# Output projections of a hybrid streaming layer: later weight pieces, and the first quarter block by block

## The chip, the cores and the metric

The kernel runs on one core of one Trainium2 chip. The metric is the device time of one execution in microseconds (us); lower is better. Instruction times below come from one profiled execution of the kernel before the change.

## What is computed

The reference is one trunk layer over 2048 prompt tokens and 32 sample tokens of another stream, with 1024 features:

```python
h = rms_norm(x, g_norm1) * (1 + scale1) + shift1
q, k, v, z, xbc_raw, dt_raw = split(h @ w_in)
attn = rms_norm(stick_breaking(norm(q), norm(k), v), g_attn_out)   # 8 heads of 64
ssm  = ssd_mixer(z, xbc_raw, dt_raw, ...)                           # 8 heads of 64, with its own rms_norm
x = x + gate1 * (concat([attn, ssm]) @ w_out)                       # the output projection
h2 = rms_norm(x, g_norm2) * (1 + scale2) + shift2
x = x + gate2 * ((silu(h2 @ w_gate) * (h2 @ w_up)) @ w_down)        # the feed-forward part, 2816 wide
```

The change concerns the line with `w_out` and its place among the work around it.

## The kernel before, in words

Every product is made of three matmuls on a high and a low part of each operand (`mm3`, lines 127 to 132). So each weight piece of 1 MB is first loaded raw into a buffer of the tag `wr` (two of them), and then split: ScalarE writes the high part `wh` and GpSimd (for `w_out` VectorE) the low part `wl`. There are three `wh`/`wl` pairs (`wtiles`, lines 72 to 78), and all the weights of the kernel take turns in them. A pair is free again when the last matmul that reads it is over.

The prompt is cut into four quarters of 512 tokens. After the input projection and the scan mixer, the stages are:

1. Attention of quarter 0, with the SSM half of quarter 0's output projection beside it (line 1605).
2. The rest of quarter 0's output projection, `run_all(w0.run())` (line 1614). It has to end before the feed-forward part can start, because that reads the normalised result `h2D` back from memory.
3. Two streams merged: `streamA` (attention of quarters 1 to 3 in `attn_w`, then `far_keys`, which adds the distant keys for those rows that need them, then the output projections of quarters 1, 2, the sample tokens and 3) and `streamF` (the feed-forward part of quarters 0 to 3).

**The order of the merged work** is set by `merge` (lines 1700 to 1726) and by a scheduler behind it. Each stream is a generator that yields a cost in nanoseconds after each piece of work it has written down. `merge` keeps a ledger: what streamA yields, times `ratio`, is owed to streamF; streamA is asked for its next piece when nothing is owed, streamF otherwise. After quarter 1's projection `ratio` is set to 4.0. The scheduler then places the instructions on the engines in about this order, each when its operands and buffers are there by its own estimate.

**The feed-forward part** (`ffn`, lines 885 to 993) goes through 11 groups per quarter. A group gets a piece of `w_gate`, of `w_up` and of `w_down`, computes two halves of 128 features (for each the products `pg` and `pu`, 24 matmuls each, yielding 5120), and then eight products `py` (6 matmuls each, yielding 1296). Pieces come from a queue (`Pieces`, lines 87 to 101) whose `get` hands out the oldest piece and at once calls for the next one. A group's `up` and `down` are thus called for when the group starts, and the next group's `gate` when its `py` start.

**One output projection** is an object `Wout` (lines 717 to 860). `pre` loads the mixed SSM rows (`mH`, `mL`), queues four pieces of `w_out` (two halves of the output columns for the SSM rows, two for the attention rows) and calls for the first (`self.pf.fill(1)`, line 735), and loads the gate rows `gr` and the residual rows `x1`. The tiles `gr` and `x1` lie in a pool on the memory that `streamA`'s attention tiles have just left. `ssm` makes the SSM products: for each half `hf`, for each of four token blocks `b`, 12 matmuls into a PSUM tile (`z`, or `d` in quarter 0), a VectorE instruction that scales it into `tm` (line 761), and a GpSimd addition into `x1` (line 763). `run` reads the attention rows, computes their norm, makes the same products for the attention half with a ScalarE sum of squares after each (line 852), and calls `norm2` for a block one block after its second half: it normalises the rows (lines 813 to 818), transposes them (line 825), writes `hx` with four ScalarE instructions for each half (line 831), splits it into `hl` and stores it to `h2D` (line 835). `hx` and `tm` share a tag of two buffers, and the two halves of `hl` have two buffers each.

`project` (lines 995 to 1000) runs `pre`, yields 3000, and then runs `ssm` and `run` for quarters 1 to 3 and for the sample tokens; quarter 0 is called from the top.

Of the kernel before, what the change touches and what calls it, by code (L numbers as in the profile page):

```python
# [35 lines left out]
def body(tc, nc, I, O):  # L36
    V, A, G, PE = nc.vector, nc.scalar, nc.gpsimd, nc.tensor
    ctx = ExitStack()
    with ctx:
# [12 lines left out]
        def load(dst, src):  # L52
            nc.sync.dma_start(dst, src)
# [73 lines left out]
        def mm3(out, pairs):  # L127
            n = len(pairs)
            for i, (sh, sl, mh, ml) in enumerate(pairs):
                PE.matmul(out, lhsT=sh, rhs=mh, start=(i == 0), stop=False)  # L130
                PE.matmul(out, lhsT=sh, rhs=ml, start=False, stop=False)  # L131
                PE.matmul(out, lhsT=sl, rhs=mh, start=False, stop=(i == n - 1))  # L132

        def mm2(out, pairs):

            n = len(pairs)
            for i, (s, mh, ml) in enumerate(pairs):
                PE.matmul(out, lhsT=s, rhs=mh, start=(i == 0), stop=False)
                PE.matmul(out, lhsT=s, rhs=ml, start=False, stop=(i == n - 1))

        def fold(dst, ps, n):
            A.activation(dst[:DEC, :n], ps[DEC:2 * DEC, :n], AF.Copy)
            V.tensor_tensor(dst[:DEC, :n], ps[:DEC, :n], dst[:DEC, :n], op=ALU.add)
# [573 lines left out]
        class Wout:  # L717
# [10 lines left out]
            def pre(self):  # L728

                s, t0 = self.s, self.t0  # L730
                mH, mL = mHL
                for i, t in enumerate((mH, mL if s == 0 else mH[:, :, DEC:])):
                    load(t[:, :, :self.n].bitcast(F32), mixT[i, :, :, t0:t0 + self.n].rearrange("k p t -> p k t"))
                self.pf = Pieces([lambda k=k, hf=hf, g=g: opiece(k, hf, g) for k, g in ((4, gsc), (0, gac)) for hf in range(2)])
                self.pf.fill(1)
                xsrc = I["x_prompt"][0, t0:t0 + self.n] if s == 0 else I["x_sample"][0]
                self.gr, self.x1 = [], {}
                for hf in range(2):
                    t = self.tile("gr", "gr")
                    load(t.rearrange("p (m c) -> p m c", m=4), modD[16 + hf * 4:20 + hf * 4, s].unsqueeze(0).to_broadcast([P, 4, P]))  # L740
                    self.gr.append(t)
                for b, c, m in self.tb:
                    x1 = self.tile("x1", "x1", nb=len(self.tb), w=D)
                    load(x1[:m], xsrc[c:c + m])
                    for hf in range(2):
                        self.x1[hf, b] = x1[:, hf * 512:(hf + 1) * 512]

            def product(self, hf, r):

                mH, mL = mHL  # L750
                wh, wl = self.pf.get()
                for b, c, m in self.tb:
                    ps = self.psum()
                    tm = self.tile("tm", "tm")
                    if self.s == 0:
                        mm3(ps[:m], [(mH[:, k, c:c + m], mL[:, k, c:c + m], wh[:, k, :], wl[:, k, :]) for k in range(4)])
                    else:
                        mm2(ps[:2 * DEC], [(mH[:, k, :2 * DEC], wh[:, k, :], wl[:, k, :]) for k in range(4)])
                        fold(tm, ps, 512)
                        ps = tm  # L760
                    V.scalar_tensor_tensor(tm[:m], ps[:m], r[:m, b:b + 1], self.gr[hf][:m], op0=ALU.mult, op1=ALU.mult)
                    x1 = self.x1[hf, b]
                    G.tensor_tensor(x1[:m], x1[:m], tm[:m], op=ALU.add)
                    yield b, tm
                    yield 12 * 216
# [72 lines left out]
            def run(self):  # L838
                yield from self.rows()
                nb, m0 = len(self.tb), self.tb[0][2]  # L840
                ra = sm.tile([P, 4], F32, tag="ra", name="ra", bufs=2)
                V.tensor_reduce(ra[:m0, :nb], stat[:m0, :, :nb].rearrange("p h b -> p b h"), axis=AX.X, op=ALU.add)
                rstd(ra[:m0, :nb], ra[:m0, :nb], 1.0 / 512, EPS)
                self.ss = {b: sm.tile([P, 2], F32, tag="s2", name="s2", bufs=8) for b, _, _ in self.tb}
                yield 1500
                lag = []
                for hf in range(2):
                    for x in self.product(hf, ra):
                        if isinstance(x, tuple):
                            b, tm = x  # L850
                            m = self.tb[b][2]
                            A.activation(tm[:m], self.x1[hf, b][:m], AF.Square, accum_out=self.ss[b][:m, hf:hf + 1])
                            continue
                        yield x
                        if hf == 1:
                            lag.append(self.tb[b])
                            if len(lag) > 1:
                                yield from self.norm2(*lag.pop(0))
                while lag:
                    yield from self.norm2(*lag.pop(0))  # L860
# [134 lines left out]
        def project(g, pool):  # L995
            w = Wout(g, pool, zps)
            w.pre()
            yield 3000
            yield from w.ssm()
            yield from w.run()  # L1000

# [597 lines left out]
        with ExitStack() as pb_:  # L1599
            mp = pb_.enter_context(tc.tile_pool(name="mp", bufs=1))  # L1600
            mHL, stat = mixed(mp)
            pw0 = ExitStack()
            w0 = Wout(0, pw0.enter_context(tc.tile_pool(name="wo0", bufs=1)), dense_ps)
            w0.pre()
            merge2(a0, w0.ssm(), R1)
            pa0.close()
            fc = px_.enter_context(tc.tile_pool(name="fc", bufs=1, side="right"))
            far_consts(fc)
            L = fc.tile([P, NH, 12], F32, name="L")
            px1 = ExitStack()  # L1610
            at1 = px1.enter_context(tc.tile_pool(name="at1", bufs=1, side="right"))
            wt = window_tiles(at1)
            a1 = chain(*(attn_w(g, at1, L, wt) for g in range(1, NQ)))
            run_all(w0.run())
            pw0.close()
            fp = pb_.enter_context(tc.tile_pool(name="fp", bufs=1))
            late = {}

            def streamA():
                yield from a1  # L1620
                yield from far_keys(at1, wt[0], L)
                px1.close()
                for g in range(1, NQ):
                    if g == 3:
                        yield from part_s()
                    with tc.tile_pool(name=f"wo{g}", bufs=1, side="right") as wo:
                        yield from project(g, wo)
                    if g < 3:
                        yield ("done", g)
                    if g == 1:  # L1630
                        yield ("ratio", 4.0)
                px_.close()
                late["ex"] = pb_.enter_context(tc.tile_pool(name="ex", bufs=1, side="right"))
                dpool[0] = pb_.enter_context(tc.tile_pool(name="pdF", bufs=5, space=PSUM))
                yield ("done", 3)

            def streamF():
                hT = load_h(0, fp, None)
                for g in range(NQ):
                    hT = yield from ffn(g, fp, late, hT)  # L1640

            merge(streamA(), streamF(), 1.55)


        fx = ctx.enter_context(tc.tile_pool(name="fx", bufs=1))
# [54 lines left out]
def merge(a, f, ratio):  # L1700
    done, debt = set(), 0.0
    a_live, f_live, need = True, True, None
    while a_live or f_live:
        blocked = a_live and need is not None and need not in done
        if not blocked:
            need = None
        if a_live and (blocked or not f_live or debt <= 0):
            try:
                c = next(a)
                if isinstance(c, tuple) and c[0] == "ratio":  # L1710
                    ratio = c[1]
                elif isinstance(c, tuple):
                    done.add(c[1])
                elif not blocked:
                    debt += c * ratio
            except StopIteration:
                a_live = False
        else:
            try:
                c = next(f)  # L1720
                if isinstance(c, tuple):
                    need = c[1]
                else:
                    debt -= c
            except StopIteration:
                f_live = False
# [29 lines left out]
```

## Time and profile before

| | us |
|---|---|
| median of three runs | 2942.09 |
| lowest, highest of the three | 2938.08, 2947.04 |
| the profiled execution | 2940.34 |
| its span, first to last instruction | 2938.4 |
| TensorE busy, of the span | 2729.8 (93%) |
| VectorE, ScalarE, GpSimd busy | 1563.9, 1186.0, 1532.6 |
| mean granted TensorE clock | 0.963 |

TensorE is busy for 93% of the span, so idle time of TensorE is what can be won, and it lies in a few places. Below, a row of the windows view gives for a stretch of time the busy microseconds of each engine with its number of instructions, then the granted TensorE clock, the busy share of the DMA engines and what they moved. A row of the timeline gives the start, the busy time (of several merged instructions where it ends in a number over x1), engine, line, operation, output and inputs, and in brackets how long the engine had been idle and what released it. `SPq` is the queue on which all these DMAs are issued.

### The profile page before, as it was taken

The page shows a single profiled execution, that of the slowest core. Times are in us where ns is not written, and L with a number is a line of the kernel's source. Part 1 is how long each engine was busy: PE and PEld are TensorE (multiplying, and loading weights), DVE is VectorE, ACT ScalarE, POOL GpSimd, SP SyncE. Part 2 cuts the span into 40 slices and gives each one's busy share as a digit, 9 for nine tenths or more (in the row PEclk, how much of TensorE's full clock was granted, in tenths as well). Part 3 has the DMA queues.
Part 4 walks back from the last instruction along what each step waited for, and adds up shares of the span by engine and source line. Part 5 has one row for each costly group of instructions (what it writes and reads, how often), then busy time and mean ns, then how long its engine had stood idle before and what let it go on. Part 6 is the DMA issues. An engine that isn't in the chain of part 4 may idle for free.

```text
span 2938.4 us, 41844 instructions
## 1 busy us (share of the span) xinstructions
PE 2729.8 (93%) x15467; PEld 2334.2 (79%) x15467; DVE 1563.9 (53%) x2575; ACT 1186.0 (40%) x2533; POOL 1532.6 (52%) x1318
## 2 busy tenths in 40 slices
PE   6998998998978689998879999999999999999998
PEld 5988997896977578876667887777787788899997
DVE  6577586766568567874344534434434422333336
ACT  6466365555535455522224334333243422322221
POOL 4767566564654635743136655544564445544445
PEclk8999998999988789999989999999999999999999
DMA  8755653463467787837745744534733722422221
GB/s 266 219 171 153 202 177 114 119 182 106 131 175 237 193 225 196 208 116 213 199 165 180 258 135 137 152 122 155 236 127 106 230 88 92 154 87 87 86 87 66
DMA packets 415619, 466.54 MB, mean 159 GB/s; under 512 B 34191, under 2 KB 330991, under 8 KB 415406
## 3 DMA queue, kind: packets, MB, share of 16 engines
q1 hardware_dynamic: 414478, 463.61, 52.7%
q8 instruction: 124, 2.03, 0.3%
q14 instruction: 89, 0.73, 0.1%
q10 hardware_dynamic: 896, 0.14, 0.0%
q0 software_dynamic: 32, 0.03, 0.0%
HBM read 372.66 MB, written 91.04 MB: 158 GB/s over the span
## 4 chain that ended last, share of the span: by engine, by line
PE 57%; DVE 6%; DMA 5%; issue 3%; POOL 2%; ACT 2%; SPq 1%; DVEq 0%; ACTq 0%; POOLq 0%
PE pg L130 5%; PE pg L131 5%; PE pg L132 5%; PE pu L130 5%; PE pu L131 5%; PE pu L132 5%; PE py L130 5%; PE py L131 4%; PE py L132 4%; PE z L130 2%; PE z L131 2%; PE z L132 1%; PE d L131 1%; PE d L130 1%; PE d L132 1%
## 5 line engine op out<-in xcount | busy, mean ns | idle before, releaser
L60 POOL TENSOR_TENSOR wl<-wr,wh 128x512 fp32r<-128x512 f32 x752 | 1010.3, 1375 | 861.7 <-ACT wh L59 778.5
L59 ACT ACTIVATE wh<-wr 128x512 fp32r<-128x512 f32 x816 | 450.3, 620 | 512.3 <-PE py L132 128.4
L130 PE MATMUL d<-wh,hH 128*128 128x256 f32 (+2 forms) x1088 | 316.0, 291 | 18.8 <-ACT hH L59 10.9
L132 PE MATMUL d<-wh,hL 128*128 128x256 f32 (+2 forms) x1088 | 311.8, 287 | 6.7 <-POOL hL L60 6.7
L130 PE MATMUL pg<-h,wh 128*128 128x512 f32 (+1 forms) x880 | 311.3, 354 | 3.7 <-POOL aT L378 2.5
L130 PE MATMUL pu<-h,wh 128*128 128x512 f32 (+1 forms) x880 | 310.5, 353 | 1.2 <-DVE sg L952 1.2
L131 PE MATMUL d<-wl,hH 128*128 128x256 f32 (+2 forms) x1088 | 311.4, 286 | 0.0
L132 PE MATMUL pg<-h,wl 128*128 128x512 f32 (+1 forms) x880 | 310.7, 353 | 0.6 <-POOL wl L60 0.6
L131 PE MATMUL pg<-h,wh 128*128 128x512 f32 (+1 forms) x880 | 310.7, 353 | 0.0
L132 PE MATMUL pu<-h,wl 128*128 128x512 f32 (+1 forms) x880 | 310.5, 353 | 0.0
L131 PE MATMUL pu<-h,wh 128*128 128x512 f32 (+1 forms) x880 | 309.9, 352 | 0.0
L130 PE MATMUL py<-wh,aH 128*128 128x512 f32 x704 | 282.5, 401 | 7.0 <-DVE ya L983 5.0
L131 PE MATMUL py<-wl,aH 128*128 128x512 f32 x704 | 277.0, 394 | 0.0
L983 DVE TENSOR_TENSOR ya<-py,ya 128x512 f32<-128x512 f32 x288 | 190.4, 684 | 148.4 <-PE py L132 146.8
L132 PE MATMUL py<-wh,aL 128*128 128x512 f32 x704 | 265.8, 394 | 2.8 <-DVE aL L60 2.8
L952 DVE TENSOR_TENSOR sg<-pg,sg 128x512 f32<-128x512 f32 (+1 forms) x110 | 64.8, 589 | 336.8 <-ACT sg L951 336.8
L130 PEld LDWEIGHTS d<-wh,hH 128*128 128x128 f32 (+1 forms) x1088 | 207.7, 191 | 23.2 <-ACT hH L59 12.5
L132 PEld LDWEIGHTS d<-wh,hL 128*128 128x128 f32 (+1 forms) x1088 | 206.9, 190 | 8.0 <-POOL hL L60 7.2
L131 PEld LDWEIGHTS d<-wl,hH 128*128 128x128 f32 (+1 forms) x1088 | 207.3, 191 | 0.7
L130 PEld LDWEIGHTS pg<-h,wh 128*128 128x128 f32 x880 | 165.6, 188 | 28.5 <-POOL aT L378 2.7
L130 PEld LDWEIGHTS pu<-h,wh 128*128 128x128 f32 x880 | 165.5, 188 | 24.2 <-DVE sg L952 1.4
L132 PEld LDWEIGHTS pg<-h,wl 128*128 128x128 f32 x880 | 165.4, 188 | 24.1 <-POOL wl L60 1.1
(434 smaller groups left out, 5686.7 us busy)
## 6 DMA issues: line engine op xcount, KB each, us to landing
wr<-in_w_in SPq DMA_DIRECT2D x48, 1024.0 KB
wr<-in_w_gate SPq DMA_DIRECT2D x44, 1024.0 KB
wr<-in_w_up SPq DMA_DIRECT2D x44, 1024.0 KB
wr<-in_w_down SPq DMA_DIRECT2D x44, 1024.0 KB
wr<-in_w_ada SPq DMA_DIRECT2D x24, 1024.0 KB
wr<-in_w_out SPq DMA_DIRECT2D x20, 1024.0 KB
h2D<-hl SPq DMA_DIRECT2D x64, 256.0 KB
Kw<-KT SPq DMA_DIRECT2D x48, 320.0 KB
```

What stands on the lines that cost most here:

```text
L59: A.activation(h, src, AF.Copy)
L60: (eng or V).tensor_tensor(l, src, h.bitcast(F32), op=ALU.subtract)
L130: PE.matmul(out, lhsT=sh, rhs=mh, start=(i == 0), stop=False)
L131: PE.matmul(out, lhsT=sh, rhs=ml, start=False, stop=False)
L132: PE.matmul(out, lhsT=sl, rhs=mh, start=False, stop=(i == n - 1))
L952: V.tensor_tensor(sg[:, :n], pg[:, :n], sg[:, :n], op=ALU.mult)
L983: V.tensor_tensor(dst, ps[:r], dst, op=ALU.add)
```

## The change

It does four things:

- `pre` calls for the first `w_out` piece only in quarter 0. In `project`, that is for quarters 1 to 3 and the sample tokens, the first piece is called for after a yield of 3500, and a second yield of 4500 follows before the SSM products, where there was one yield of 3000.
- In quarter 0, `run` takes both attention pieces of `w_out` from the queue at once and makes the products block by block: both halves of block 0, then of block 1, and so on. Before, all blocks of the first half came ahead of those of the second.
- `product` accepts a piece and a list of blocks for that.
- The ratio with which `merge` starts is 1.45 where it was 1.55.

```diff
@@ pre
                 self.pf = Pieces([lambda k=k, hf=hf, g=g: opiece(k, hf, g) for k, g in ((4, gsc), (0, gac)) for hf in range(2)])
-                self.pf.fill(1)
+                if self.g == 0:
+                    self.pf.fill(1)
@@ product
-            def product(self, hf, r):
+            def product(self, hf, r, w=None, tb=None):
 
                 mH, mL = mHL
-                wh, wl = self.pf.get()
-                for b, c, m in self.tb:
+                wh, wl = w or self.pf.get()
+                for b, c, m in tb or self.tb:
@@ run
                 lag = []
-                for hf in range(2):
-                    for x in self.product(hf, ra):
+                if self.g == 0:
+                    work = [self.pf.get() for _ in range(2)]
+                    work = [(hf, self.product(hf, ra, work[hf], [tb])) for tb in self.tb for hf in range(2)]
+                else:
+                    work = [(hf, self.product(hf, ra)) for hf in range(2)]
+                for hf, p in work:
+                    for x in p:
@@ project
             w.pre()
-            yield 3000
+            yield 3500
+            w.pf.fill(1)
+            yield 4500
             yield from w.ssm()
             yield from w.run()
@@ body
-            merge(streamA(), streamF(), 1.55)
+            merge(streamA(), streamF(), 1.45)
```

## The prediction

> **What bounds the kernel now.** First the page, for the share of each engine, then the windows view for where TensorE is not busy.
>
> ```profile
> span 2938.4 us, 41844 instructions
> ...
> PE 2729.8 (93%) x15467; PEld 2334.2 (79%) x15467; DVE 1563.9 (53%) x2575; ACT 1186.0 (40%) x2533; POOL 1532.6 (52%) x1318
> ```
>
> ```profile
> 1009.00:1048.00 39.00, 15.61 (x74) 12.68 (x72) 20.45 (x35) 25.89 (x60) 13.62 (x16) 0.60 0.89 266
> ...
> 1315.00:1402.00 87.00, 78.32 (x367) 62.27 (x366) 32.55 (x54) 21.33 (x44) 32.04 (x24) 1.00 0.74 198
> ...
> 1402.00:1460.00 58.00, 52.01 (x230) 41.11 (x228) 22.58 (x42) 12.91 (x26) 5.22 (x4) 0.94 0.81 230
> ...
> 1460.00:1496.00 36.00, 17.08 (x41) 10.22 (x40) 16.36 (x30) 0.26 (x1) 0.00 (x0) 0.65 0.54 182
> ...
> 1517.00:2925.00 1408.00, 1393.26 (x7065) 1165.89 (x7064) 561.61 (x848) 459.22 (x938) 722.14 (x571) 1.00 0.42 136
> ```
>
> TensorE works 2729.8 of 2938.4 us, so only idle time can be won. After 1517 it is idle for 14.7 us in 1408; before about 900 the change touches nothing. Two stretches are left. From 1009 to 1048 it works 15.6 of 39 us at a clock of 0.60: the end of quarter 0's output projection, for which the feed-forward part waits. From 1315 to 1496 it works 147 of 181 us: `far_keys` and the start of quarter 1's projection, with 19 of the 34 idle us in the last 36. Next I read that place in the queue of DMA issues, in ScalarE's timeline and in TensorE's.
>
> ```profile
> 1341.74 0.53 SPq L53 DMA_DIRECT2D wr<-in_w_gate  x1
> ...
> 1354.81 0.54 SPq L53 DMA_DIRECT2D wr<-in_w_up  x1
> ...
> 1377.58 0.52 SPq L53 DMA_DIRECT2D wr<-in_w_down  x1
> ...
> 1388.51 0.54 SPq L53 DMA_DIRECT2D wr<-in_w_out  x1
> ...
> 1403.17 0.54 SPq L53 DMA_DIRECT2D wr<-in_w_out  x1
> ...
> 1421.04 0.44 SPq L53 DMA_DIRECT2D wr<-in_w_gate  x1
> ...
> 1438.21 0.54 SPq L53 DMA_DIRECT2D wr<-in_w_out  x1
> ...
> 1451.49 0.78 SPq L53 DMA_DIRECT2D wr<-in_w_up  x1
> ```
>
> ```profile
> 1401.88 0.60 ACT L951 ACTIVATE sg<-pg 128x512 f32<-128x512 f32 x1 [1.96 <-PE pg L132]
> ...
> 1416.94 2.55 ACT L114 ACTIVATE wh<-wr,cols 128x512 fp32r<-128x512 f32 x4
> ...
> 1424.78 2.56 ACT L114 ACTIVATE wh<-wr,cols 128x512 fp32r<-128x512 f32 x4 [4.81 <-issue]
> ...
> 1445.03 2.19 ACT L59 ACTIVATE wh<-wr 128x512 fp32r<-128x512 f32 x4 [6.74 <-PE py L132]
> ...
> 1459.26 0.60 ACT L951 ACTIVATE sg<-pg 128x512 f32<-128x512 f32 x1 [1.89 <-PE pg L132]
> ...
> 1504.58 2.57 ACT L114 ACTIVATE wh<-wr,cols 128x512 fp32r<-128x512 f32 x4 [36.69 <-PE z L132]
> ...
> 1515.68 2.20 ACT L59 ACTIVATE wh<-wr 128x512 fp32r<-128x512 f32 x4 [0.99 <-PE z L132]
> ```
>
> ```profile
> 1495.27 1.41 DVE L761 SCALAR_TENSOR_TENSOR tm<-z,rsS,gr 128x512 f32<-128x512 f32 x2 [6.14 <-DMA gr<-modD]
> ...
> 1496.08 0.79 PE L130 MATMUL z<-wh,mH 128*128 128x512 f32 x1 [8.00 <-DVE tm L761]
> ...
> 1502.23 0.40 PE L130 MATMUL z<-wh,mH 128*128 128x512 f32 x1
> ...
> 1502.94 0.39 PE L130 MATMUL z<-wh,mH 128*128 128x512 f32 x1
> ...
> 1516.88 0.39 PE L130 MATMUL pu<-h,wh 128*128 128x512 f32 x1
> ...
> 1517.34 0.39 PE L130 MATMUL pg<-h,wh 128*128 128x512 f32 x1
> ```
>
> The raw pieces come in this order: `gate`, `up` and `down` of feed-forward group 7 (counted from 0; 1341.7 to 1377.6), two pieces of `w_out`, `gate` of group 8, a third piece of `w_out`, `up` of group 8. ScalarE shows how the three split pairs go round. The two `w_out` pieces (line 114) take the pairs that `gate` and `up` of group 7 leave, at 1416.9 and 1424.8; `gate` of group 8 gets the third at 1445.0, when the `py` are over. The third `w_out` piece is split at 1504.6, when the first has served its four SSM products, and `up` of group 8 at 1515.7, when the second has. So the feed-forward part ends its first `pg` of group 8 at 1459.3 (the sigmoid that reads it) and has nothing until `pu` at 1516.9. The second `pg` of that group needed only `gate`, there since 1445, yet it starts at 1517.3, after `pu`: the products of one PSUM tag are placed in the order of the program. What holds the two pieces is the first SSM product's scaling, which TensorE awaited for 8.0 us before 1496.1: it waited in turn for `gr` (1495.3), whose memory is free only when `far_keys` is over.
>
> **The change part by part.** *Quarter 0 block by block.*
>
> ```profile
> 985.41 1.41 DVE L761 SCALAR_TENSOR_TENSOR tm<-d,ra,gr 128x512 f32<-128x512 f32 x2 [1.14 <-POOL ra L150]
> ...
> 997.30 0.75 DVE L761 SCALAR_TENSOR_TENSOR tm<-d,ra,gr 128x512 f32<-128x512 f32 x1 [1.68 <-PE d L132]
> ...
> 1003.98 0.75 DVE L761 SCALAR_TENSOR_TENSOR tm<-d,ra,gr 128x512 f32<-128x512 f32 x1 [1.28 <-ACT tm L852]
> ...
> 1009.42 1.23 DVE L813 TENSOR_TENSOR s<-s 128x1 f32<-128x1 f32 x1
> ...
> 1019.74 0.74 DVE L761 SCALAR_TENSOR_TENSOR tm<-d,ra,gr 128x512 f32<-128x512 f32 x1
> ...
> 1030.80 0.74 DVE L761 SCALAR_TENSOR_TENSOR tm<-d,ra,gr 128x512 f32<-128x512 f32 x1
> ...
> 1033.34 9.40 SPq L56 DMA_DIRECT2D h2D<-hl  x8
> ...
> 1045.33 9.76 SPq L53 DMA_DIRECT2D h<-h2D  x16
> ...
> 1048.26 0.77 PE L130 MATMUL pg<-h,wh 128*128 128x512 f32 x1 [2.50 <-POOL aT L378]
> ```
>
> ```profile
> L763 POOL TENSOR_TENSOR x<-x,tm 128x512 f32<-128x512 f32 x3 | 4.2, 1413 | 10.9 <-DVE tm L761 10.9
> ...
> L852 ACT ACTIVATE tm<-x 128x512 f32<-128x512 f32 x3 | 1.9, 619 | 0.3 <-POOL x L763 0.3
> ```
>
> The eight attention products are scaled at line 761; the fourth at 997.3, the sixth at 1004.0. Only then may `norm2` of block 0 begin, at 1009.4 (line 813), as the sixth product is the second half of block 1. From there a chain of four `norm2` runs to the last stores of `h2D` (1033.3 to 1042.7), the read back at 1045.3 and the first `pg` at 1048.3. The last two products are scaled inside it, at 1019.7 and 1030.8, long after TensorE made them, because `tm` shares its two buffers with `hx`. Block by block, block 1's second half is the fourth product instead of the sixth. If `norm2` follows the last product that is called ahead of it by the same 5.4 us (1004.0 to 1009.4), it starts at 1002.7, 6.7 earlier; if it needs block 0 alone, at about 997, 12.4 earlier. I take 8.5. Given back: two more products are scaled and added inside the chain, up to 2 x (1.4 + 0.6) = 4 us (the second row pair's means), partly under the wait for the stores; I take 2. That is **-6.5**, between 0 and -12. The matmuls are the same. Holding both halves delays the splits of the first `up` and `down`, which take the pairs released by the two pieces: these would come at about 1010 instead of 997 and 1009, under the chain, which still has 25 us to go; without that cover one split, some 6 us, would show.
>
> *The ratio.* Up to the end of `far_keys` streamA yields 74.2 thousand (three times 24.74) in attention and 66.4 in `far_keys`, 140.6 in all. At 1.45 the feed-forward part is given 0.10 x 74.2 = 7.4 thousand less by the end of the attention. A step of 5120 is 24 matmuls; three take 0.71 us (1502.23 to 1502.94), one 0.235, a step 5.6. So `far_keys` starts 8.1 us earlier, and as much feed-forward work is left for later. This gains only what waiting for `far_keys` costs.
>
> *The order of the pieces.* This decides. Before, the first `w_out` piece was called for when the ledger stood at 140.6 x 1.55 = 217.9; seven feed-forward groups make 7 x 30.85 = 215.9, so group 7 had started and its three pieces were called for. That is the order of the queue's rows. Now the ledger stands at (140.6 + 3.5) x 1.45 = 208.9 at the first piece and at 148.6 x 1.45 = 215.4 at the second, both short of 215.9: only `gate` of group 7 (called for at 205.6, where the `py` of group 6 start) is ahead. The later yields move the pieces 8.0 x 1.45 = 11.6 along, but the lower ratio has moved the feed-forward part back by 14.1. The new order: `gate` of 7, `w_out`, `w_out`, `up`, `down`, `w_out`, `gate` of 8. With three pairs, `up` of group 7 gets one only when the first `w_out` piece has served its four products. So the feed-forward part is held at the first `pg` of group 7, which was over at 1401.9, instead of that of group 8, over at 1459.3. Queued behind the hold are the `pu`, the second `pg` and all `py` of group 7; who waits is TensorE.
>
> How long?
>
> ```profile
> L59 ACT ACTIVATE fh<-t x7: 384/385/386, 1331.6 to 1457.0; 128x256 fp32r<-128x256 f32 x7
> ```
>
> The seven chunks of `far_keys` come every (1457.0 - 1331.6) / 6 = 20.9 us, and 4.4 were done at 1401.9. Now 8.1 / 20.9 = 0.4 more are done at the same step, which comes at 1401.9 - 6.5 + 2 (the extra chunk's matmuls) = 1397.4. The 2.2 that are left run without rival weights. From 1402 to 1460 the DMA engines moved 230 x 58 = 13.3 MB, 4.2 of it four weight pieces; the rest is 2.9 chunks of 3.15 MB (by the code's tiles). At 230 GB/s a chunk takes 13.7 us; one weight piece more falls into the stretch. Ends: 13.7 and 20.9; I take 15.7, near the first, since the loads that shared the queue are gone. The last chunk is then split at 1397.4 + 2.2 x 15.7 = 1432. From there `pu` came 59.9 us later before; 11.3 of that were the second four SSM products (48 x 0.235), not needed now: 1480.5. Before, the feed-forward part resumed at 1516.9, but with more done: 144 matmuls of group 7 and 8 (33.8 us) and the four products (11.3). So that state is reached at 1525.6, **+8.7** with the quarter-0 gain in it.
>
> A rule bears on the 15.7. TensorE's clock was 0.65 from 1460 to 1496, and a matmul took 0.79 us at 1496.1 and 0.40 at 1502.2. The Trainium skill (TensorE: Matmul & The Clock Gate, "HAM oscillation") warns against idle gaps over some 3.4 us, as the clock is then halved; the trace agrees. By an estimate from that rule all of the 2.2 chunks' matmuls (8 of 512 columns, 16 of 256) would take twice their time. I leave it out of the sum, as a chunk waits for its keys; if its matmuls lay on the chain, it would be rival 2. The skill's DMA: Bandwidth & Descriptors ("Measured") has 341 GB/s for loads of 1 MB. By that estimate a chunk would take 9.2 us and the sum would be 2936; the 230 GB/s at a DMA share of 0.81 speak against it.
>
> *The later quarters.* In quarter 2 the first piece now follows `up` and `down` of its group, and at ratio 4.0 the sample tokens' and quarter 3's follow further feed-forward groups. There are 14.7 idle us after 1517; I take **-2**, between -6 and +4 (pieces that come late would hold streamA, which nobody awaits before quarter 3's end).
>
> Sum: 2940.3 + 8.7 - 2 = **2947**, against the profiled execution, which lies 1.8 under the median of 2942.1.
>
> **The rivals.** (1) The feed-forward part isn't held at that `pg`: the second `pg` passes `pu`, and one pair in turn serves `gate`, `up` and `down`. Against it: 1517.3. For it: TensorE had other work queued there. Then both gains count: `far_keys` ends 6.5 + 8.1 = 14.6 us earlier, less 5 for the waits on single splits and one step: 2940.3 - 9.6 - 2 = 2929. (2) Slower: `far_keys` alone doesn't quicken, because keys are issued as TensorE frees their two buffers, not as the DMA engines allow. Price: 2.2 x (20.9 - 15.7) = 11.4, so 2959. It decides from a pace of 17 us, where the sum passes 0.3%. The same end comes if the clock stays near 0.65 for the whole hold and the chunks' matmuls lie on the chain: 2.2 x (8 x 0.235 + 16 x 0.118) = 8.3 more, 2955. For it: four DMA issues for every key tile, and that clock; against it: the 13.3 MB add up. (3) The norm chain keeps its end, because two more products wait in `tm`: 2954. That the change leaves the order of the loads as it was is ruled out by the ledger.
>
> **How the numbers follow.** About 0.3% (8.8 us) is what a measurement of this kernel can tell from no change. My forecast, 2947 with a range of its own from 2936 to 2958: chance 0.46 (0.33 within 0.3%, 0.11 slower, 0.02 faster). Rival 1: 0.30 (0.23 faster, 0.07 within). Rival 2: 0.16 (0.15 slower, 0.01 within). Rival 3: 0.08 (0.06 slower, 0.02 within). Together faster 0.25, same 0.43, slower 0.32. The range of 8 in 10 takes in the middle of rival 1 and rival 2: 2924 to 2964.
>
> **What would show it.** In the profile after: line 813 first runs under 1003 and the first `pg` at about 1042; the queue issues `w_out` twice between `gate` and `up` of group 7; TensorE has a gap of some 80 us with only `far_keys` and SSM matmuls, then `pu` of group 7; the chunks' splits come closer together in it. I am wrong if `pu` of group 7 runs before the SSM products, or if the chunks keep 21 us.

## The result, and the profile after

The changed kernel takes 2983.94 us (median of 4 runs, 2978.20 to 2988.29) against 2944.57 for the kernel before on the same chip (4 runs, 2938.08 to 2948.27). The ratio is 1.0135, interval 1.0108 to 1.0162: 39 us slower, where 2947 and a range up to 2964 had been forecast. The profiled execution has a span of 2976.4 us, 38.0 more than before.

The page of the changed kernel first, then its windows: columns as before, with 2050 to 2160 as a stretch of its own.

```profile
span 2976.4 us, 41833 instructions
...
PE 2738.1 (92%) x15467; PEld 2337.5 (79%) x15467; DVE 1539.1 (52%) x2575; ACT 1184.9 (40%) x2533; POOL 1532.4 (51%) x1318
```

```profile
1009.00:1048.00 39.00, 19.42 (x71) 14.93 (x70) 16.82 (x28) 23.99 (x57) 15.42 (x17) 0.57 0.92 275
...
1402.00:1460.00 58.00, 31.72 (x90) 20.87 (x89) 12.53 (x30) 3.87 (x11) 0.00 (x0) 0.64 0.59 158
...
2050.00:2160.00 110.00, 89.30 (x374) 69.01 (x373) 50.00 (x74) 35.72 (x71) 63.65 (x50) 0.91 0.65 219
```

The kernel before had in the last of these stretches:

```profile
2050.00:2160.00 110.00, 108.03 (x483) 86.63 (x482) 49.27 (x70) 37.92 (x74) 64.75 (x52) 1.00 0.62 209
```

TensorE is busy for 8.3 us more, so 29.7 of the 38.0 us of span are idle time. It comes in two places, with 20.3 and 18.7 us more idle time than before; other stretches give some back. From 1402 to 1460 TensorE works 31.7 us instead of 52.0, for 90 matmuls instead of 230, at a clock of 0.64: that is the hold that was forecast. From 2050 to 2160 it works 89.3 of 110 us instead of 108.0: nothing in the prediction stands for that. From 1009 to 1048, where quarter 0's term was to be won, it does much the same as before (71 matmuls, 74 before).

**The first place.** The queue's order, ScalarE's split of `up` of group 7 and TensorE's return:

```profile
1339.64 0.54 SPq L53 DMA_DIRECT2D wr<-in_w_gate  x1
...
1357.64 0.53 SPq L53 DMA_DIRECT2D wr<-in_w_out  x1
...
1376.04 0.54 SPq L53 DMA_DIRECT2D wr<-in_w_out  x1
...
1388.28 0.39 SPq L53 DMA_DIRECT2D wr<-in_w_up  x1
...
1398.98 0.38 SPq L53 DMA_DIRECT2D wr<-in_w_down  x1
```

```profile
1404.20 0.60 ACT L957 ACTIVATE sg<-pg 128x512 f32<-128x512 f32 x1
1409.10 0.38 ACT L59 ACTIVATE fh<-t 128x256 fp32r<-128x256 f32 x1 [4.29 <-PE t L594]
...
1429.88 0.38 ACT L59 ACTIVATE fh<-t 128x256 fp32r<-128x256 f32 x1 [2.67 <-PE t L594]
...
1450.33 0.38 ACT L59 ACTIVATE fh<-t 128x256 fp32r<-128x256 f32 x1 [4.82 <-PE t L594]
...
1493.89 2.19 ACT L59 ACTIVATE wh<-wr 128x512 fp32r<-128x512 f32 x4 [34.44 <-PE z L132]
```

```profile
1486.68 0.79 PE L130 MATMUL z<-wh,mH 128*128 128x512 f32 x1 [7.23 <-DVE tm L762]
...
1496.49 0.39 PE L130 MATMUL pu<-h,wh 128*128 128x512 f32 x1
```

`gate` of group 7, two pieces of `w_out`, then `up` and `down`: as forecast. The sigmoid at 1404.2 reads the first `pg` of group 7; the three `fh` are the last three chunks of `far_keys`, 20.8 and 20.5 us apart; `up` of group 7, loaded at 1388.3, is split only at 1493.9, after waiting for `z`, and `pu` runs at 1496.5. That is 16 us later than the 1480.5 of the prediction. The window of the last two intervals:

```profile
1409.10:1450.30 41.20, 22.72 (x62) 15.28 (x62) 4.77 (x12) 2.08 (x6) 0.00 (x0) 0.56 0.61 162
```

TensorE is idle for 18.5 of these 41.2 us; by the view of its waits it waited 11.2 us for keys and 4.9 us for values, while the DMA engines were busy for 0.61 of the time and the clock was 0.56.

**The second place.** The passage of the feed-forward part from quarter 1 to quarter 2: queue, GpSimd and TensorE. Line numbers are those of the changed kernel; in the feed-forward part they are higher than before by up to 6.

```profile
2089.58 9.53 SPq L53 DMA_DIRECT2D h<-h2D  x13
...
2100.71 0.42 SPq L53 DMA_DIRECT2D mH<-mixT  x1
...
2102.31 1.08 SPq L53 DMA_DIRECT2D xf<-x1D  x1
```

```profile
2099.17 1.30 POOL L930 TENSOR_TENSOR ya<-ya,xf 128x512 f32<-128x512 f32 x1
...
2111.28 6.21 POOL L60 TENSOR_TENSOR wl<-wr,wh 128x512 fp32r<-128x512 f32 x5 [5.32 <-ACT wh L59]
2117.45 1.26 POOL L930 TENSOR_TENSOR ya<-ya,xf 128x512 f32<-128x512 f32 x1
...
2137.08 1.26 POOL L930 TENSOR_TENSOR ya<-ya,xf 128x512 f32<-128x512 f32 x1 [13.01 <-DMA xf<-x1D]
```

```profile
2107.70 0.68 PE L826 MATMUL t<-ident,xn 32*128 32x32 f32 x8
2121.33 0.80 PE L130 MATMUL pg<-h,wh 128*128 128x512 f32 x1 [12.95 <-DVE yt L992]
```

In the last group of quarter 1 each `py` is scaled into `yt` (line 992) and added to a `ya` to which GpSimd has first added the residual rows `xf` (line 930). There is one `xf` tile, read again only after each addition. The addition at 2117.5, the fourth of eight, starts 18.3 us after the one before. So `yt` cannot be emptied, the PSUM buffers of `py` (the memory that holds its products) stay taken, and the first `pg` of quarter 2 waits 13.0 us for line 992. Before, the SSM products of quarter 3 were under way there: 119 `z` matmuls from 2050 to 2160, 43 after, and none of those between 2107.7 and 2121.3. In the new order `mH` of quarter 3 is only read at 2100.7.

The kernel before has such a pause too (line 924 is its line 930):

```profile
2086.01 1.30 POOL L924 TENSOR_TENSOR ya<-ya,xf 128x512 f32<-128x512 f32 x1 [6.55 <-DMA xf<-x1D]
...
2105.49 1.29 POOL L924 TENSOR_TENSOR ya<-ya,xf 128x512 f32<-128x512 f32 x1
```

Its 19.5 us come behind the fourth addition instead of the third, the first `pg` of quarter 2 runs at 2096.1, inside the pause, and from 2094.5 to 2108 TensorE is busy for 11.7 of 13.5 us, with 23 `z` matmuls among 49. So the pause itself is not new; what is new is that it comes one addition sooner and that TensorE has nothing else to do in it.

### The profile page after: what moved, and what is told of

Read it like the earlier page. It is cut to its first block, busy times and chain, and to the rows that moved or that the text cites. A ratio compares the mean times of both kernels' runs of the same rounds, so it can differ in the third digit from the quotient of the medians.

```text
span 2976.4 us, 41833 instructions
## 1 busy us (share of the span) xinstructions
PE 2738.1 (92%) x15467; PEld 2337.5 (79%) x15467; DVE 1539.1 (52%) x2575; ACT 1184.9 (40%) x2533; POOL 1532.4 (51%) x1318
## 4 chain that ended last, share of the span: by engine, by line
PE 60%; DMA 6%; DVE 5%; POOL 2%; issue 2%; ACT 2%; SPq 1%; DVEq 0%; ACTq 0%; POOLq 0%
PE pg L130 5%; PE pg L131 5%; PE pg L132 5%; PE pu L130 5%; PE pu L132 5%; PE pu L131 5%; PE py L130 5%; PE py L131 4%; PE py L132 4%; PE z L130 2%; PE z L131 2%; PE z L132 2%; PE d L131 1%; DMA Vf<-VS 1%; PE d L130 1%
## 5 line engine op out<-in xcount | busy, mean ns | idle before, releaser
L130 PE MATMUL pg<-h,wh 128*128 128x512 f32 (+1 forms) x880 | 312.3, 355 | 22.2 <-DVE yt L992 18.7
L130 PEld LDWEIGHTS pg<-h,wh 128*128 128x128 f32 x880 | 166.2, 189 | 48.0 <-DVE yt L992 19.2
L963 DVE TENSOR_TENSOR sg<-pu,sg 128x512 f32<-128x512 f32 (+1 forms) x110 | 65.1, 591 | 253.8 <-PE pu L132 252.8
L131 PEld LDWEIGHTS pg<-h,wh 128*128 128x128 f32 x880 | 166.7, 189 | 23.6
```

The lines of the kernel that those rows point to most:

```text
L963: V.tensor_tensor(sg[:, :n], pu[:, :n], sg[:, :n], op=ALU.mult)
```

## The experiments

Ratios are to the kernel before, run on the same chip; 0.3% is 8.8 us.

| kernel | median us | ratio (interval) | span of its profile |
|---|---|---|---|
| 1 before, quarter 0 block by block | 2949.34 | 1.0009 (0.9994 to 1.0023) | 2940.4 |
| 2 before, ratio 1.45 | 2964.12 | 1.0061 (1.0047 to 1.0075) | 2958.4 |
| 3 changed, late yields for quarter 1 alone | 2963.12 | 1.0060 (1.0044 to 1.0075) | 2959.8 |
| 4 changed, ratio 1.55 | 2954.09 | 1.0025 (1.0013 to 1.0036) | 2946.5 |
| 5 changed, no residual in quarter 1 | 2962.07 | 1.0066 (1.0042 to 1.0090) | 2954.8 |
| 6 changed, third key tile | 2966.60 | 1.0074 (1.0047 to 1.0100) | 2964.6 |
| 7 changed, quarter 1 alone, 9000 | 2938.10 | 0.9982 (0.9965 to 0.9998) | 2933.3 |
| 8 number 1 with four buffers | 2936.61 | 0.9977 (0.9960 to 0.9993) | 2928.5 |
| 9 before, four buffers | 2938.71 | 0.9985 (0.9965 to 1.0004) | 2932.3 |
| 10 before, third key tile | 2932.92 | 0.9955 (0.9939 to 0.9971) | 2932.2 |
| 11 numbers 7, 8 and the third key tile | 2923.99 | 0.9930 (0.9914 to 0.9947) | 2927.2 |
| 12 number 11, pieces behind group 8 | 2940.87 | 0.9983 (0.9961 to 1.0005) | 2953.4 |

**1. Quarter 0 block by block, alone.** The edit is the part of the change's diff in `product` and `run`, on the kernel before.

> The kernel before with nothing of the change but quarter 0's attention products block by block. Theory A (all of the time goes into two stalls of TensorE elsewhere, and the norm chain of quarter 0 keeps its end: its last read of h2D was issued at 1044.95 after and at 1045.33 before): within 2 us of the kernel before, first pg of the feed-forward part within 1 us of 1048.3. Theory B (the term of the prediction holds and was only buried): 6.5 us faster, first pg at 1042.

No difference: 1.0009. Line 813, in VectorE's timeline, at the first and the last call of `norm2`, and the first `pg`:

```profile
996.62 0.15 DVE L813 TENSOR_TENSOR s<-s 128x1 f32<-128x1 f32 x1
...
1034.12 0.16 DVE L813 TENSOR_TENSOR s<-s 128x1 f32<-128x1 f32 x1 [2.24 <-ACT tm L857]
```

```profile
1048.57 0.47 PE L130 MATMUL pg<-h,wh 128*128 128x512 f32 x1 [3.10 <-POOL aT L378]
```

The chain starts at 996.6 instead of 1009.4 and its last call comes at 1034.1 instead of 1034.0. Theory A holds.

**2. The ratio alone.**

```diff
-            merge(streamA(), streamF(), 1.55)
+            merge(streamA(), streamF(), 1.45)
```

> The kernel before with nothing of the change but the ratio 1.45. Its loads have one w_out piece between gate and up of group 7, the second only behind down, and both first pieces of quarter 3 ahead of the read of h for quarter 2. Theory A (a stall at group 7 because two w_out pieces and one gate hold all three split pairs, a second one at the passage from quarter 1 to quarter 2 of the feed-forward part because no output projection covers it): neither stall is there, so from 6 us faster to 4 us slower than the kernel before. Theory B (the smaller ratio is the cost: feed-forward work is missing beside far_keys and left over at the end): 20 us or more slower.

Neither number came: 18 us slower, with the first stall and without the second. The windows, and the queue around group 7:

```profile
1402.00:1460.00 58.00, 32.45 (x95) 22.20 (x94) 9.40 (x23) 3.62 (x10) 0.00 (x0) 0.61 0.59 166
...
2050.00:2160.00 110.00, 108.94 (x478) 87.07 (x478) 53.57 (x68) 34.31 (x65) 67.85 (x49) 1.00 0.61 203
```

```profile
1340.04 0.54 SPq L53 DMA_DIRECT2D wr<-in_w_out  x1
...
1357.84 0.53 SPq L53 DMA_DIRECT2D wr<-in_w_gate  x1
...
1375.92 0.54 SPq L53 DMA_DIRECT2D wr<-in_w_out  x1
...
1391.09 0.39 SPq L53 DMA_DIRECT2D wr<-in_w_up  x1
```

The expectation looked only at what lies between `gate` and `up` of group 7, and overlooked that the first piece of `w_out` stands ahead of `gate` (1340.0). Two pieces and one `gate` are again ahead of `up`, they hold all three pairs, and the stall at 1402 is that of the changed kernel (32.5 of 58 us). From 2050 to 2160 TensorE is busy for 108.9 of 110. So the ratio alone makes the first stall, through the order of the pieces, and costs 18 us; the later yields, which move the pieces back, do not move them far enough.

**3. The later yields for quarter 1 alone.**

```diff
-                if self.g == 0:
+                if not (self.g == 1):
                     self.pf.fill(1)
...
-            yield 3500
-            w.pf.fill(1)
-            yield 4500
+            if g == 1:
+                yield 3500
+                w.pf.fill(1)
+                yield 4500
+            else:
+                yield 3000
```

> The changed kernel, but the later yields only for quarter 1; quarters 2, 3 and the sample tokens call for their first piece in pre and yield 3000 again. The loads around group 7 stay as changed; at the read of h for quarter 2 the projection of quarter 3 is under way again. Theory A: the stall at group 7 stays (about 20 us, 1402 to 1460), that of 2100 to 2120 goes (20.7 us of idle TensorE between 2050 and 2160 become about 2): 16 to 20 us faster than the changed kernel, so 18 to 23 us slower than the kernel before. Theory B (one cause, at group 7, and the gap at 2100 only a consequence of it): the gap stays and the time is that of the changed kernel, 38 us slower than before.

```profile
1402.00:1460.00 58.00, 31.12 (x86) 20.75 (x84) 8.21 (x21) 3.72 (x10) 0.00 (x0) 0.59 0.60 164
...
2050.00:2160.00 110.00, 109.90 (x477) 87.95 (x476) 49.99 (x67) 31.89 (x63) 69.42 (x53) 1.00 0.61 201
```

The first stall stays, the second is gone (109.9 of 110 us busy); 18 us slower than before instead of 39. Theory A holds. So the later yields of the quarters behind quarter 1 cost about 22 us (1.0135 less 1.0060), by the spans 16.6, and the first stall about 18: the two make the result. The additions of `xf` come without the long pause here, 6.7 to 11.1 us apart: quarter 3's products stand ahead of the last `py` and among them, and five of the eight additions are made when the first `py` is scaled (2120.8).

**4. All of the change at ratio 1.55** (`merge(streamA(), streamF(), 1.55)` in the changed kernel).

> The changed kernel with the ratio 1.55. Around group 7 the loads stand as before (gate, up, down, then two w_out); at the read of h for quarter 2 the sample tokens' last piece comes behind it and quarter 3's projection two groups later. Theory A: the stall at group 7 goes, so TensorE is busy for about 50 of 58 us after far_keys' fourth chunk as before, and the stall at the read of h stays, perhaps smaller by the few products of the sample tokens: 13 to 20 us slower than the kernel before. Theory B (the ratio is the cost): within 4 us of the kernel before.

```profile
1402.00:1460.00 58.00, 50.30 (x216) 39.92 (x215) 21.20 (x40) 12.05 (x24) 4.95 (x4) 0.91 0.81 224
...
2050.00:2160.00 110.00, 100.22 (x423) 76.35 (x422) 54.90 (x63) 39.22 (x77) 64.65 (x50) 0.98 0.66 221
```

7 us slower (1.0025), between the two theories. The first stall is gone, as theory A has it. The second is there with half its size, 9.8 us idle of 110 instead of 20.7: 16 `z` matmuls of the sample tokens run in this stretch, and none of quarter 3's. A's 13 to 20 was too much, and with the ratio back the later yields still cost.

**5. No residual rows in quarter 1.** In `residual`, the read of `xf` and its addition (lines 913 to 930) are skipped for `g == 1`, so the output of quarter 1 lacks these rows.

```diff
+                    if g == 1:
+                        xl_.append(None)
+                        return
                     xt = (ex or fp).tile([P, 512], F32, tag="xf", name="xf", bufs=nx)
...
-                    G.tensor_tensor(dst[:m], dst[:m], xl_[i][:m], op=ALU.add)
+                    if g != 1:
+                        G.tensor_tensor(dst[:m], dst[:m], xl_[i][:m], op=ALU.add)
```

> The changed kernel, but in quarter 1 the feed-forward part leaves out the addition of the residual rows xf and their reads (the output lacks them); nothing else differs. Theory A (from 2107.7 to 2121.3 TensorE waits because the last products py cannot be read out: VectorE waits for GpSimd's addition of xf, the only xf tile is read again only after each addition, and each of these reads stands in the queue behind 4 MB of h and more weights): the idle time between 2050 and 2160 falls from 20.7 us to under 6, 14 to 18 us faster than the changed kernel, 1.007 to 1.009 of the kernel before. Theory B (the first pg of quarter 2 waits for the rows of h itself): the idle time stays within 3 us of 20.7, about 1.013 of the kernel before.

```profile
2050.00:2160.00 110.00, 109.07 (x478) 85.61 (x477) 49.03 (x77) 43.95 (x85) 62.70 (x48) 1.00 0.62 209
```

The gap closes, although `h` is read no sooner (from 2090.7 on) and the products of quarter 3 do not fill it (their first runs at 2134.2): 0.9 us idle instead of 20.7, and 21.6 us less in the span. The first `pg` of quarter 2 runs at 2110.4, 11 us sooner and without a wait. So the `h` rows are not what is waited for. Whether the read of `xf` or GpSimd's queue comes last is not told apart: ahead of the addition at 2117.5, GpSimd was splitting `wl` from 2111.3 on.

**6. A third key tile**, in the memory of the tag `Q` that attention has left, so that three tiles of keys are on their way.

```diff
-                    Ks = at_.tile([P, 2, 640], F32R, tag="Kw", name="Kf", bufs=2)...
+                    if len(klist) % 3 == 1:
+                        Ks = [at_.tile([P, 512], F32R, tag="Q", name="Kq", bufs=2)... for _ in range(2)]
+                    else:
+                        Ks = at_.tile([P, 2, 640], F32R, tag="Kw", name="Kf", bufs=2)...
...
             for f in (kget, vget):
                 f()
                 f()
+            kget()
```

> The changed kernel with a third key tile for far_keys (in memory that attention has left), so that three tiles of keys are on their way instead of two; the same matmuls and bytes. Theory A (with the feed-forward part held, the pace of a chunk is the latency of its four key tiles through two buffers): the chunks' pace falls from 20.7 us to 14 to 17, the last one is split at about 1430 instead of 1450, the feed-forward part resumes some 15 to 20 us earlier; 1.006 to 1.009 of the kernel before. Theory B (the DMA queue as a whole, 0.59 busy there, or the halved clock sets the pace): pace 19 to 21 us, about 1.013 of the kernel before.

The last three chunks, from ScalarE's timeline, with the sigmoid of the first `pg` of group 7 and the split of its `up`, and the window of 1402 to 1460:

```profile
1404.68 0.38 ACT L59 ACTIVATE fh<-t 128x256 fp32r<-128x256 f32 x1 [6.57 <-PE t L599]
...
1413.92 0.60 ACT L962 ACTIVATE sg<-pg 128x512 f32<-128x512 f32 x1 [0.74 <-PE pg L132]
...
1416.88 0.38 ACT L59 ACTIVATE fh<-t 128x256 fp32r<-128x256 f32 x1 [2.37 <-PE t L599]
...
1437.01 0.38 ACT L59 ACTIVATE fh<-t 128x256 fp32r<-128x256 f32 x1 [4.84 <-PE t L599]
...
1482.82 2.20 ACT L59 ACTIVATE wh<-wr 128x512 fp32r<-128x512 f32 x4 [36.66 <-PE z L132]
```

```profile
1402.00:1460.00 58.00, 38.88 (x140) 26.62 (x139) 22.71 (x44) 5.88 (x13) 0.00 (x0) 0.82 0.69 210
```

The last chunk is split 13.3 us sooner (1437.0 instead of 1450.3) and `up` of group 7 11.1 us sooner, less than the 15 to 20 that were expected. By the medians the gain is 18 us, by the spans 11.8; the latter fits the split. Theory A's time came, but its reason is not shown. The hold starts 9.7 us later here, at 1413.9, and the chunks that come closer together do so ahead of it: the one at 1404.7 follows 15.4 us after the chunk before (split at 1389.3), the next one 12.2 us later, while the feed-forward part still runs. Inside the hold there is one interval, 20.1 us, and the same one took 20.5 in the changed kernel. In it the granted clock was 0.75 instead of 0.62, and 2 MB of `up` and `down` were read as well (issued from 1427.5 on), so it speaks neither for the two key tiles nor for the queue.

**7. Quarter 1's pieces behind `up` and `down`, ratio 1.45.** As number 3, but `yield 9000` instead of `yield 3500`.

> The changed kernel at its ratio of 1.45, with the later yields only for quarter 1 and there 9000 and 4500 instead of 3500 and 4500, so that both first w_out pieces of quarter 1 come behind up and down of group 7, as in the kernel before, and those of quarter 3 ahead of the read of h for quarter 2. Theory A (the order of the pieces at the three split pairs is what costs at group 7, not the ratio): TensorE is busy for 48 us or more of 1402 to 1460 instead of 31.7, and the time is within 5 us of the kernel before. Theory B (the smaller ratio costs by itself, as the kernel with the ratio alone was 18 us slower): about 18 us slower than the kernel before, 1.006.

```profile
1402.00:1460.00 58.00, 52.83 (x239) 42.06 (x237) 22.95 (x42) 12.96 (x26) 8.42 (x7) 0.97 0.79 226
...
2050.00:2160.00 110.00, 107.38 (x478) 85.47 (x477) 48.75 (x66) 36.72 (x72) 61.49 (x49) 1.00 0.59 199
```

Both stalls are gone at the ratio of the change, and the kernel is 5 us faster than before (0.9982). Theory A holds: it is the order, not the ratio.

**8 and 9. Four buffers in quarter 0's projection**, with and without the block order:

```diff
             def tile(self, tag, name, dt=F32, nb=2, w=512):
+                nb = 4 if self.g == 0 else nb
```

> The kernel before with quarter 0's attention products block by block and four buffers instead of two for each tag of quarter 0's projection. Block by block alone, the chain of norm2 began 12.8 us earlier (line 813 at 996.6 instead of 1009.4) and ended at the same time (1034.1, 1034.0). Theory A (its middle waits for buffers: tm shared with hx, hl until its store has left): the last line 813 moves to 1022 to 1028, the first pg to 1037 to 1042, 6 to 11 us faster than the kernel before. Theory B (its middle waits for GpSimd and ScalarE, which split up and down there, and for the steps themselves): the first pg stays within 3 us of 1048, the time within 3 us of the kernel before.

> The kernel before, its attention products half by half as they were, with four buffers instead of two for each tag of quarter 0's projection and nothing else. Theory A (the buffers and the block order are worth something only together, because half by half the sixth product has to come before the first norm2): from 5 us faster to no change. Theory B (the buffers alone are the bound of that stage, the block order adds nothing): 8 to 11 us faster, as with both.

The last `norm2` and the first `pg` with both, and then the same with four buffers alone:

```profile
1022.44 0.14 DVE L814 TENSOR_TENSOR s<-s 128x1 f32<-128x1 f32 x1
```

```profile
1046.67 0.73 PE L130 MATMUL pg<-h,wh 128*128 128x512 f32 x1
```

```profile
1021.73 0.15 DVE L814 TENSOR_TENSOR s<-s 128x1 f32<-128x1 f32 x1
```

```profile
1045.83 0.76 PE L130 MATMUL pg<-h,wh 128*128 128x512 f32 x1 [2.62 <-DMA h<-h2D]
```

With four buffers the chain ends at 1022 instead of 1034, so it was held by buffers. The time falls by 6.8 us with the block order (0.9977) and by 4.4 without (0.9985, an interval that takes in no change). The intervals overlap: what the block order adds is not told apart. The place was wrong: the first `pg` comes at 1046.7 and 1045.8, not at 1037 to 1042. In number 8 the read of `h` is issued from 1039.2 on, 6.1 us sooner, behind loads of attention (`Q`, `Vw`, `Kw` from 1035.6 on), and in number 9 the first `pg` waits for `h`. What came earlier was the work of attention: TensorE makes 84 and 81 of its matmuls between 1009 and 1048 instead of 40, and the first chunk of `far_keys` is split at 1319.1 and 1322.8 instead of 1331.6.

**10. The third key tile in the kernel before.**

> The kernel before with nothing but the third key tile in far_keys. Theory A (the feed-forward part is held until far_keys is over and the SSM products are made, so whatever ends far_keys sooner ends the hold sooner): the last chunk is split 8 to 13 us before 1457, 5 to 12 us faster than the kernel before. Theory B (with the feed-forward part running beside it, the keys come at the pace that TensorE and the shared queue allow): within 3 us of the kernel before.

```profile
L59 ACT ACTIVATE fh<-t x7: 357/384/387, 1334.6 to 1442.4; 128x256 fp32r<-128x256 f32 x7
```

The last chunk is split at 1442.4 instead of 1457.0, and the kernel is 13 us faster (0.9955): theory A, a little above its numbers. Here the feed-forward part runs beside the chunks up to the last one, so this does not show how fast they come in a hold.

**11. The three together.**

> Three parts together: the changed kernel with the late pieces only for quarter 1 and behind up and down of group 7 (9000 and 4500, ratio 1.45), quarter 0 block by block with four buffers, and the third key tile. Theory A (three separate costs): 7 us from the first, 9 from the second, and 3 to 10 from the third, where the feed-forward part still stands between 1460 and 1496: 16 to 26 us faster than the kernel before. Theory B (the first two are the same idle time won twice, and the third only reaches the next hold sooner): 8 to 12 us faster.

```profile
1460.00:1496.00 36.00, 19.74 (x58) 12.80 (x59) 13.21 (x23) 0.60 (x1) 3.82 (x3) 0.67 0.75 262
```

21 us faster than the kernel before (0.9930; 15 to 25 by the interval): theory A. The parts alone give 5, 7 and 13, together 25, each of them uncertain by some 5 us, so whether something is won twice is not told apart. This is the fastest kernel here. From 1460 to 1496 it is still held.

**12. The pieces behind group 8**: in number 11, ratio 1.50, and `yield 24000` and `yield 3000` for quarter 1.

> As the combined kernel, but with ratio 1.50 and 24000 and 3000 for quarter 1, so that both first w_out pieces come behind up and down of group 8: no weight of the feed-forward part waits for an SSM product while far_keys runs. Theory A (what is left between 1460 and 1496 is the hold at the split pairs): TensorE is busy for over 32 of 36 us there, and the time is 5 to 15 us below the combined kernel's, unless the projection of quarter 1 then ends after the feed-forward part asks for it. Theory B (the end of quarter 1's projection or the passage to quarter 2 takes it back): the time of the combined kernel or more, with the idle time near group 10 of quarter 0 or at the read of h.

```profile
1460.00:1496.00 36.00, 32.25 (x132) 25.46 (x131) 18.91 (x30) 6.76 (x11) 0.00 (x0) 0.95 0.56 185
```

```profile
1650.44 0.79 PE L130 MATMUL pg<-h,wh 128*128 128x512 f32 x1 [12.98 <-DMA h<-h2D]
```

The hold is filled (32.3 of 36 us busy), and theory B takes it back: quarter 1's projection ends later (the read of `h` that follows it is issued from 1647.4 on instead of 1625.1), and at the passage to quarter 1 TensorE waits 13.0 us for `h`, from 1600 to 1680 it works 57.6 of 80 us instead of all 80. The time is that of the kernel before (the profiled execution, at 2954.83 us, lies above the median).

## Why the prediction was wrong, step by step

**Quarter 0, -6.5: nothing came.** The chain started 13 us earlier, a little more than its upper case of 12.4; 8.5 were taken. The step that failed is the 2 us taken for what is given back ("two more products are scaled and added inside the chain"). All was given back, because the middle of the chain waits for buffers (numbers 1, 8 and 9), and the read of `h2D` came 0.4 us earlier. That was rival 3, at 0.08. A second assumption would have failed too, that the first `pg` follows the end of the chain: in number 8 a chain that ends 12 us sooner moves it by 1.6 us.

**The order of the pieces: right.** The ledger gave the order of the loads exactly, and with it the hold at the first `pg` of group 7 that starts with the wait for the pairs and ends with the fourth SSM product. Numbers 2, 4 and 7 show that the stall comes and goes with this order. That it is the three pairs through which the order acts rests on the trace (the split of `up` waits for `z` at 1493.9); a fourth pair was not tried. Rival 1, that the feed-forward part is not held, is out.

**The length of the hold: the mis-sized term is the 15.7 us per chunk.** It was taken near the 13.7 of a shared queue that is freed; measured were 20.6 in the mean, as before the change (20.9), with the queue 0.61 busy. So the step "the loads that shared the queue are gone" does not give a faster chunk. The last chunk came at 1450.3 instead of 1432: 6.8 of this from the first `pg` of group 7, whose sigmoid ran at 1404.2 and not at 1397.4 (quarter 0's 6.5 were missing), the other 11.5 from the pace. From there to `pu` passed 46.2 us, 48.6 were taken. Rival 2 named the size (11.4) and the sign ("the chunks keep 21 us"). Its mechanism, the two key buffers, stays open: TensorE did wait for keys and values beside a queue that was not full, but number 6 has no quicker interval inside its hold. Its other condition, the lower clock with the matmuls on the chain (8.3), stays open as well, as no run holds the clock apart.

On the clock the trace shows 0.64 in the hold after 0.65 before; the `z` matmul at 1486.7 took 0.79 us behind 7.2 idle us, `pu` at 1496.5 took 0.39. This goes with the Trainium skill (TensorE: Matmul & The Clock Gate, "HAM oscillation"), which warns against idle gaps of over some 3.4 us.

In the stretch of the hold the queue moved 158 GB/s. The Trainium skill's DMA: Bandwidth & Descriptors ("Measured") has 341 GB/s for a transfer of 1 MB and 138 for one of 64 KB, of loads issued from GpSimd; the prediction's estimate of 9.2 us a chunk took the first. The keys are read 128 KB at a time and from another queue, so neither row was measured for them, and no run here shows what the size of a load does.

**The later quarters, -2 between -6 and +4: wrong in sign and size, 17 to 22 us lost.** The step that failed is "pieces that come late would hold streamA, which nobody awaits before quarter 3's end". Nobody awaits it, but TensorE lives on it: at the passage between two quarters the feed-forward part waits for its own residual rows (number 5), and the SSM products of quarter 3 were what TensorE did meanwhile (number 3, and the same pause in the kernel before). The prediction put quarter 3's pieces behind further feed-forward groups, but did not ask what this leaves TensorE at the passage, where `mH` is now read behind `h`; it looked at 14.7 idle us after 1517 and not at what kept them so few. No rival had this place.

In sum, by profiled executions, for which 2947 was worked out: `pu` of group 7 came 16.0 us later than predicted (6.8 and 11.5, less 2.4 for the shorter way to `pu`), and the 2 of the later quarters were not there. That makes 2965; number 3, which has this stall alone, ran its profile in 2961.70, and the 3 us between are not traced. By its median of 2963.12 it still lies just inside the range up to 2964. The second stall, 16.6 us by the spans, for which the forecast had no term, leads from there to 2978.20, the profiled execution of the changed kernel.

## What to carry to other kernels

Before work is moved, ask what it covers where it is now, as well as whom it holds: a stream that nobody awaits can still be the only thing an engine has to do during another stream's wait. With a small ring of shared buffers, write down the order of the requests across the edit, to the piece, since two requests ahead of the critical one cost 18 us here. And when other loads leave a queue, do not take the pace of those that stay from the queue's rate without a trace in which the queue is full: here they kept 20.6 us a chunk at a DMA share of 0.61.

## What the runs showed of the hardware

With the feed-forward part's loads gone, the reads of `far_keys` moved 162 GB/s at a DMA share of 0.61 between 1409 and 1450. That is not the queue's limit, since the same queue moved 4 MB of `h` with more at 270 GB/s and a share of 0.78 between 2090 and 2160. A read of 256 KB, `xf` issued at 2129.28 behind 3.5 MB that were issued from 2122.1 on (the rows of `x`, a `gate` piece and `ao`), let GpSimd start only at 2137.08. And in number 8 a chain that ended 12 us sooner moved the first `pg` by 1.6 us, while the kernel gained 7: TensorE made more of attention's matmuls in that stretch, and the first chunk of `far_keys` came 12.6 us sooner.
